# Norms row by row, and a second layer's first operands made on chip, in a hybrid encoder layer

## The chip, the cores and the metric

The kernel runs on one core of a Trainium2 chip. The metric is the device time of one execution in microseconds (us), lower is better. The program is written in a tile framework: Python generators issue instructions, the framework fixes at build the order of each engine's instructions, near to the order in which the generators are stepped, and adds the waits. The engines are TensorE (PE in the profile; PEld its weight loads), the vector engine (DVE), ScalarE (ACT), GpSimd (POOL), and SyncE's queue (SP), which issues nearly all DMAs and, in order, waits for what each transfer needs.

## The reference

One layer over two sequences (512 and 1024 rows of 1024 numbers), with alpha = 2^0.25:

```python
x = layer_norm(ALPHA * x + 0.5 * swiglu(x, ffn1_wg, ffn1_wu, ffn1_wd), ln_g[0], ln_b[0])
x = layer_norm(ALPHA * x + hybrid_mixer(x, w_in, ..., w_out), ln_g[1], ln_b[1])
x = layer_norm(ALPHA * x + 0.5 * swiglu(x, ffn2_wg, ffn2_wu, ffn2_wd), ln_g[2], ln_b[2])

def swiglu(x, wg, wu, wd):            # 1024 -> 2816 -> 1024
    return (silu(x @ wg) * (x @ wu)) @ wd

def hybrid_mixer(h, ...):
    rx, rgate, q, k, v, fx = split(h @ w_in)
    out_a = gelu(rgate) * bidir_rglru(conv(rx))
    out_b = diff_attention(q, k, v)             # four heads, two maps each
    out_c = fourier_mix(fx)                     # Re of a 2-D DFT per channel group
    return concat(out_a, out_b, out_c) @ w_out
```

`layer_norm` subtracts a row's mean, divides by the root of its variance plus 1e-5, multiplies by a gain and adds a bias, all over the 1024 numbers of a row. Everything is fp32.

## The kernel before

The 1536 rows are 12 row tiles of 128 x 1024. The FFNs work in two halves of 6 row tiles; the mixer in three chunks of 4 (chunk 0 is the first sequence). Rows between the parts (`x1` after FFN1, `x2` after the mixer) lie in DRAM.

**Products.** An fp32 product is three matmuls on a high and a low part of each operand (`mm3`, L138). `split` makes the parts: ScalarE casts the high one (L132), the vector engine subtracts it (L133).

**An FFN (`ffn`, L321 on)** makes 11 passes over the 2816 hidden columns, 256 in each, once for each half. A pass has 14 up products: the gate (m = 0) and the up weight (m = 1) in Strassen's scheme of seven products over quarters (`up`). The products' right operands are sums of transposed quarters of the half's rows, 7 operands in three column blocks, made in 21 steps by `seven`: a vector sum, 4 transposes into an accumulator bank (L263), a split. FFN1's first half makes them on chip from its input (`operands`). For each other half they are staged: 21 stores into DRAM (`operands_to`), then loads into the six "xt" slots (`operands_from`). The left operands are sums of weight blocks, made by the vector engine in a first pass of each half (`Weights.made`), three products ahead (`PREP`); from the second pass of the second half on they are loaded, as made in the first half (`kept`, two by two). The down products (`down`, `down_seven`) of a pass stand between the up products of the next.

**The norms.** `layer_norm` (L210 on) takes rows in batches of up to four: means, squares with their sum on ScalarE (L225), one small vector step (L227), a power -0.5 on GpSimd (L228); then for each row (x + mean) * gain on the vector engine (L231); then for odd rows the scale and bias in one vector multiply (L238), and for even rows a scale on ScalarE (L235) and an addition on GpSimd (L236). A first half's norm runs in the second half's first pass, in two batches of three; a second half's runs at the end behind each row's last down product, row by row.

**The mixer (L1209 on).** `project` multiplies by `w_in`; its left columns are transposes of `x1` rows (`columns`; chunk 0's were staged at the end of FFN1, chunks 1 and 2 load their rows from DRAM). Then come the recurrence and, block by block, the attention, beside which `others` is stepped: the rest of `project`, the Fourier parts (`fnet`) of both sequences, the output projections (`out_proj`) of chunks 0 and 1 and the norm of chunk 0. At the end stand, in this order:

```python
norm(1, accs[1])
run(islice(staging, len(SEVEN)))
for _ in self.out_proj(2, chunk(x1, 2), accs[2]):
    next(staging, None)
run(staging)
norm(2, accs[2])
```

where `staging` loads the rows of `x2` that FFN2's first half needs ("p" slots), makes its operands and stores them. An output projection has 16 output tiles, each of 24 matmuls of 256 columns, drained by the vector engine into the residual rows, which are in "x" slots (six in all); the norm of chunk 1 works on four of them.

Of the kernel before, what the change touches and what calls it, by code (L numbers as in the profile page):

```python
# [67 lines left out]
STREAM = 2  # L68
DOWN_AT = (0, 1, 3, 4, 6, 8, 9, 11)
# [33 lines left out]
class Kernel:  # L103
# [137 lines left out]


# [78 lines left out]
    def ffn(self, n, which, src, dst, scr, wscr, first=False, beside=iter(()), staged=iter(()), meanwhile=iter(())):  # L321
# [108 lines left out]

        def out(m, got, i, j, x, result):
# [80 lines left out]
        def norm(half, accs, parts):  # L512
            params = self.ln_params(which, "p")
            for part in parts:
                self.layer_norm(accs, sums[:, half] if half else sums[:, half, :, :1], params, dst[half * HALF:(half + 1) * HALF], part)
                yield
# [15 lines left out]
        def kept(todo):  # L532

            slots, views = [], []

            def ahead(n=STREAM):
                while todo and len(slots) < n:
                    w = self.slot("w", [2, 2, h, P], F32R)
                    nc.sync.dma_start(f32(w), f32(todo.pop(0)))
                    slots.append(w)  # L540
# [10 lines left out]

        def first_pair(raws, rooms):
# [4 lines left out]
        ready = iter(())  # L557
        if first:
            rows = self.load_rows(src[:HALF], "x")
            raws = load(0)  # L560
            _, store, operand = self.operands()
            ready = self.seven(lambda r: rows[r::3], store, [(k, r) for k in SEVEN for r in range(3)], nc.gpsimd)
        else:
            raws = load(0)
# [5 lines left out]
        staging = self.operands_to(self.pairs(src[HALF:]), scr[1], [(k, r) for r in range(3) for k in SEVEN])  # L570
# [7 lines left out]
        with self.phase(f"ffn{n}a", FFN_SLOTS, FFN_BANKS):  # L578
            run(islice(ready, 6))
            for p in range(NP):  # L580
# [5 lines left out]
                else:  # L586
                    products = both(first_pair(raws, [[t[:, 0], t[:, 1]] for t in (self.slot("p", [2, h, P]) for _ in raws)]), got, "h")
# [8 lines left out]
                if p == 0:  # L596
                    accs = self.load_rows(src[:HALF], "x")
# [5 lines left out]
            operand = self.operands_from(scr[1])  # L603
# [3 lines left out]
        norms = norm(0, accs, [range(0, 3), range(3, 6)])  # L607
        get, ahead = kept([wscr[p][:, c:c + 2] for p in range(1, NP) for c in range(0, 2 * len(SEVEN), 2)])

        def between():  # L610
            if p == 0:
                next(norms, None)
            if STAGE <= p:
                next(staging, None)

        with self.phase(f"ffn{n}b", LATE_SLOTS, LATE_BANKS):
            steps = iter(())
            for p in range(NP):
                got = {}
                result = "a" if p == NP - 1 else None  # L620
                if p:
                    fifth = lambda: self.slot("d", [HT])
                    products = chain(*(up(m, get, got, between, result, fifth) for m in range(2)))
                else:
                    products = both(first_pair(raws, [[self.slot(t, [h, P]) for t in "bd"] for _ in raws]), got, result)
# [19 lines left out]
            norms = norm(1, accs, [range(t, t + 1) for t in last])  # L645
            for t in last:
                next(meanwhile, None)
                down(got, ws, t, True)
                next(norms)
            run(meanwhile)  # L650

# [490 lines left out]
    def run(self):  # L1142
        tc, nc, ins = self.tc, self.nc, self.ins
        with ExitStack() as ctx:
# [45 lines left out]
            scr = [[[dram.tile([P, KD // 2, 2, HT], F32R, name=f"ops{n}{i}{k}") for k in SEVEN] for i in range(2)] for n in range(2)]  # L1190
# [107 lines left out]
```

## Time and profile before

| | us |
|---|---|
| three runs, median | 2902.63 (2901.74 to 2905.0) |
| the profiled execution, its own time | 2902.0 |
| its span | 2899.9 |
| TensorE busy | 2762.1 (95%) |
| vector engine busy | 1929.5 (67%) |
| ScalarE busy | 1157.9 (40%) |
| GpSimd busy | 135.1 (5%) |

The mean granted TensorE clock is 0.976 of full speed. The span is what the profiler saw between the first and the last instruction; the execution's own time has 2.1 us more. Busy times are unions over an engine's instructions, and a wait is put down to the semaphore that came last. On the time axis FFN1's first half ends at about 546 us, FFN1 at 1070, the attention's first sequence lies from about 1410 to 1530, the mixer ends at 1859 with FFN2's first pass behind it, and FFN2's second half begins at about 2383.

### The profile page before, as it was taken

How to read it: one execution, taken by the hardware profiler on the slowest of the kernel's cores; microseconds unless marked ns; L12 is line 12 of the kernel's file. 1: busy time of each engine (PE TensorE's matmuls, PEld its weight loads, DVE VectorE, ACT ScalarE, POOL GpSimd, SP SyncE). 2: the span in 40 equal slices, each digit the busy share in tenths (PEclk: the TensorE clock that was granted, in tenths of full speed). 3: DMA queues.
4: the chain of work that ended last, by engine and by line, in shares of the span. 5: the costliest groups of instructions: out<-in, count | busy, mean ns of one | idle time of the engine just before them, and what ended most of it. 6: DMA issues, size and time to landing. Idle time of an engine off the chain costs nothing. (4 is left out here: it accounts for less than half of the span.)

```text
span 2899.9 us, 39216 instructions
## 1 busy us (share of the span) xinstructions
PE 2762.1 (95%) x14940; PEld 2521.3 (87%) x14940; DVE 1929.5 (67%) x3217; ACT 1157.9 (40%) x2093; POOL 135.1 (5%) x106
## 2 busy tenths in 40 slices
PE   8999999899999989999889986899999998999997
PEld 7999999799999978978678976799999998999996
DVE  7677666677676672453477754667766667676776
ACT  5344334333332344662365642344443334323223
POOL 2000000100000020000000011100000001000002
PEclk9999999999999999999899998899999999999999
DMA  7799766878555572244585486988876586555552
GB/s 255 267 317 317 281 239 227 302 282 271 198 183 193 183 241 83 96 159 141 171 235 153 136 277 216 339 291 303 296 280 242 211 310 221 201 187 191 190 186 104
DMA packets 318076, 650.48 MB, mean 224 GB/s; under 512 B 22976, under 2 KB 194624, under 8 KB 297408
## 3 DMA queue, kind: packets, MB, share of 16 engines
q1 hardware_dynamic: 313888, 641.16, 64.0%
q0 software_dynamic: 4000, 6.82, 0.9%
q8 instruction: 117, 1.92, 0.3%
q14 instruction: 71, 0.58, 0.1%
HBM read 403.06 MB, written 244.84 MB: 223 GB/s over the span
## 5 line engine op out<-in xcount | busy, mean ns | idle before, releaser
L138 PE MATMUL up<-xt,a 128*128 128x384 f32 x4032 | 746.8, 340 | 36.9 <-ACT a L132 27.3
L138 PEld LDWEIGHTS up<-xt,a 128*128 128x128 f32 x4032 | 710.8, 190 | 52.5 <-ACT a L132 31.8
L138 PE MATMUL up<-xt,w 128*128 128x384 f32 x3360 | 617.9, 337 | 0.0
L138 PEld LDWEIGHTS up<-xt,w 128*128 128x128 f32 x3360 | 588.6, 188 | 22.3 <-ACT t L422 10.0
L138 PE MATMUL big<-w,h 128*128 128x512 f32 x1584 | 387.1, 393 | 0.5 <-ACT h L132 0.2
L509 DVE SCALAR_TENSOR_TENSOR x<-big,x 128x512 f32<-128x512 f32 x420 | 277.7, 685 | 111.7 <-PE big L138 109.0
L138 PEld LDWEIGHTS big<-w,h 128*128 128x128 f32 x1584 | 295.3, 188 | 58.7 <-ACT h L132 1.6
L138 PE MATMUL big<-a,h 128*128 128x512 f32 x1260 | 317.9, 394 | 0.0
L138 PEld LDWEIGHTS big<-a,h 128*128 128x128 f32 x1260 | 234.0, 188 | 40.7
L138 PE MATMUL big<-xt,w 128*128 128x512 f32 x1008 | 234.3, 392 | 0.0
L456 DVE SCALAR_TENSOR_TENSOR x<-big,x 128x1024 f32<-128x1024 f32 (+1 forms) x156 | 177.2, 1138 | 81.0 <-PE big L138 78.5
L138 PEld LDWEIGHTS big<-xt,w 128*128 128x128 f32 x1008 | 189.7, 189 | 40.2 <-ACT x L961 0.4
L133 DVE TENSOR_TENSOR a<-w,a 128x512 fp32r<-128x512 f32 x244 | 166.2, 698 | 50.2 <-ACT a L132 48.4
L132 ACT CAST a<-w 128x512 fp32r<-128x512 f32 x244 | 147.6, 621 | 22.3 <-DMA w<-in_ffn_wg 14.0
L132 ACT CAST a<-b 128x512 fp32r<-128x512 f32 x168 | 103.8, 620 | 122.0 <-PE up L138 50.5
L133 DVE TENSOR_TENSOR a<-b,a 128x512 fp32r<-128x512 f32 x168 | 114.9, 688 | 42.9 <-ACT a L132 40.5
L132 ACT CAST h<-t 128x384 fp32r<-128x384 f32 x168 | 86.2, 513 | 119.5 <-DVE t L439 72.3
L138 PE MATMUL mm<-w,xt 128*128 128x256 f32 x960 | 122.4, 285 | 1.3 <-DVE x L1136 1.3
L138 PEld LDWEIGHTS mm<-w,xt 128*128 128x128 f32 x960 | 118.2, 193 | 2.0 <-DVE x L1136 1.9
L403 DVE TENSOR_TENSOR t<-t,up 128x384 f32<-128x384 f32 x88 | 48.7, 553 | 91.7 <-ACT t L402 91.3
L422 ACT COPY t<-up 128x384 f32<-128x384 f32 x88 | 42.2, 479 | 166.6 <-PE up L138 166.4
L414 ACT COPY t<-up 128x384 f32<-128x384 f32 x88 | 42.2, 479 | 161.8 <-PE up L138 161.8
(309 smaller groups left out, 3129.8 us busy)
## 6 DMA issues: line engine op xcount, KB each, us to landing
left<-a SPq DMA_DIRECT2D x280, 512.0 KB, 4.2
w<-left SPq DMA_DIRECT2D x140, 1024.0 KB, 4.7
ops<-a SPq DMA_DIRECT2D x63, 512.0 KB, 4.2
x<-x SPq DMA_DIRECT2D x52, 512.0 KB, 4.3
w<-in_ffn_wg SPq DMA_DIRECT2D x24, 1024.0 KB, 5.8
w<-in_ffn_wu SPq DMA_DIRECT2D x24, 1024.0 KB, 7.4
d<-in_ffn_wd SPq DMA_DIRECT2D x88, 256.0 KB, 4.5
w<-in_ffn_wd SPq DMA_DIRECT2D x20, 1024.0 KB, 5.0
```

The costliest lines, as they stand in the source:

```text
L132: self.nc.scalar.copy(hi, src)
L133: self.nc.vector.tensor_sub(lo, src, f32(hi))
L138: self.nc.tensor.matmul(out, lhs(l), rhs(r), start=first and n == 0, stop=last and n == 2, skip_group_check=onto)
L403: nc.vector.tensor_add(s, s, b)
L414: nc.scalar.copy(s, a)
L422: nc.scalar.copy(s2 := quarter(), a)
L456: nc.vector.scalar_tensor_tensor(accs[t][:, at], pd, scale, accs[t][:, at], op0=ALU.mult, op1=ALU.add, **acc)
L509: nc.vector.scalar_tensor_tensor(x, ps, scale, x, op0=ALU.mult, op1=ALU.add)
```

## The change

1. **Norms row by row.** `layer_norm_row` does one row in three steps, all multiplies on the vector engine, and `layer_norm_rows` interleaves neighbours. It is used for both halves of both FFNs and for chunks 1 and 2. Chunk 0's norm stays a batch.
2. **FFN2's first operands on chip.** Rows 0 to 3 of `x2` are loaded into the mixer's "m" slots, rows 4 and 5 are those of chunk 1 in their "x" slots. 18 of the 21 steps of `seven` are stepped with chunk 2's output projection, three in FFN2's first pass. Chunk 1's norm goes row by row beside that projection (rows 2, 3, 0, 1), chunk 2's goes along with FFN2's first pass (`extra`).
3. **The FFNs' end.** The last pass's up products for m = 1 go in the order 1, 2, 3, 4, 5, 0, 6 (`up_late`), the rows' last down products in the order 3, 4, 5, 0, 1, 2, and the first of them comes before the last up products.
4. **FFN1 into the mixer.** FFN1's last six rows stay in their slots (`held`); of chunk 1 only rows 4 and 5 are loaded, into "a" slots.
5. **Fourier.** The first step of each `fnet` (loads and vector folds) is stepped earlier, between the steps of `project`.
6. Rooms for weight sums are in "b" and "d" slots in the first halves too (before: "p"), and the mixer's norm parameters in "p" (before: "x").

```diff
+    def layer_norm_row(self, a, sums, params, dst):
...
+        nc.vector.tensor_scalar(mean, sums, -1.0 / D, None, op0=ALU.mult)
+        nc.scalar.activation(self.slot("a", [D], BF16), a, AF.Square, bias=mean, accum_out=var)
+        yield
+        nc.vector.tensor_scalar(var, var, 1.0 / D, EPS / ALPHA ** 2, op0=ALU.mult, op1=ALU.add)
+        nc.gpsimd.tensor_tensor(rs, var, self.mhalf[:, :1], op=ALU.pow)
+        nc.vector.scalar_tensor_tensor(a, a, mean, params[0], op0=ALU.add, op1=ALU.mult)
+        yield
+        nc.vector.scalar_tensor_tensor(a, a, rs, params[1], op0=ALU.mult, op1=ALU.add)
+        nc.sync.dma_start(dst, a)
+        yield
+    def layer_norm_rows(self, rows, params):
+        late = iter(())
+        for x in rows:
+            row = self.layer_norm_row(*x[:2], params, x[2])
+            next(row)
+            next(late, None)
+            yield
+            next(row)
+            late = row
+            yield
+        next(late, None)
+        yield
@@ ffn @@
+        def ending(got, ws):
+            norms = norm(1, accs, last)
+            for t in last:
+                down(got, ws, t, True)
+                next(norms)
+                next(norms)
+                next(meanwhile, None)
+                yield
+            run(norms)
-        if first:
+        if start is None:
...
-            operand = self.operands_from(scr[0])
+            operand, ready, extra = start
...
-        last = (3, 0, 1, 2, 4, 5)
+        last = (3, 4, 5, 0, 1, 2)
@@ first half, first pass @@
                 for i, _ in enumerate(products):
+                    if not p:
+                        next(extra, None)
                     if not p and i % 2:
                         run(islice(ready, 3))
@@ second half @@
-        norms = norm(0, accs, [range(0, 3), range(3, 6)])
+        norms = norm(0, accs, last)
...
                 for i, _ in enumerate(products):
+                    if p == 0:
+                        next(norms, None)
                     if i in DOWN_AT:
                         next(steps, None)
+                    if p == NP - 1 and i == 12:
+                        run(steps)
+                        rest = ending(got, ws)
+                        next(rest)
@@ run @@
-            xts = [self.columns_from(cols)] + [self.columns(lambda c=c: self.load_rows(chunk(x1, c), "x")) for c in range(1, NCH)]
+            held = []
+            xts = [self.columns_from(cols), self.columns(lambda: self.load_rows(x1[TPC:HALF], "a") + held[:2 * TPC - HALF]),
+                   self.columns(lambda: held[2 * TPC - HALF:])]
@@ mixer @@
-        order = [(k, r) for r in range(3) for k in SEVEN]
-        staging = self.operands_to(self.pairs(x2[:HALF]), scr, order)
-        others = Steps(project, self.fnet(0, SEQS[0]), self.fnet(1, SEQS[1]),
+        fnets = [self.fnet(q, S) for q, S in enumerate(SEQS)]
+        others = Steps(islice(project, 15), begun(fnets[0]), project, islice(fnets[0], 3), begun(fnets[1]), *fnets,
                        self.out_proj(0, chunk(x1, 0), None, beside=x1p), first_norm(),
                        self.out_proj(1, chunk(x1, 1), accs[1]))
         along(self.attention(blocks[0] + blocks[1], dist, others), others, PACE)
-        norm(1, accs[1])
-        run(islice(staging, len(SEVEN)))
-        for _ in self.out_proj(2, chunk(x1, 2), accs[2]):
-            next(staging, None)
-        run(staging)
-        norm(2, accs[2])
+        rows = self.load_rows(x2[:TPC], "m") + accs[1][:HALF - TPC]
+        params = self.ln_params(1, "p")
+        norms = norm(1, accs[1], params, (2, 3, 0, 1))
+        _, store, operand = self.operands()
+        ready = self.seven(lambda r: rows[r::3], store, [(k, r) for k in SEVEN for r in range(3)], nc.vector)
+        for n, _ in enumerate(self.out_proj(2, chunk(x1, 2), accs[2])):
+            next(norms, None)
+            if n >= 8:
+                run(islice(ready, 1 + n % 2))
+        run(norms)
+        return operand, ready, norm(2, accs[2], params)
```

**Where the order moves.** First TensorE, from the end of chunk 2's output projection (`mm<-w,xt`) over the transposes of the operands (`big<-ident`) into FFN2's first pass (`up`) with the first down products behind it (`big<-w,h`). Before:

```order
L263 MATMUL big<-ident,p 128x128 x4
L138 MATMUL mm<-w,xt 128x256 x24
L263 MATMUL big<-ident,p 128x128 x4
L138 MATMUL mm<-w,xt 128x256 x144
L138 MATMUL up<-xt,a 128x384 x168
L138 MATMUL big<-w,h 128x512
L138 MATMUL up<-xt,a 128x384 x2
```
With the change:

```order
L139 MATMUL mm<-w,xt 128x256 x24
L297 MATMUL big<-ident,x 128x128 x8
L139 MATMUL up<-xt,a 128x384 x24
L297 MATMUL big<-ident,m 128x128 x8
L139 MATMUL up<-xt,a 128x384 x12
L297 MATMUL big<-ident,m 128x128 x4
L139 MATMUL up<-xt,a 128x384 x98
L139 MATMUL big<-w,h 128x512
L139 MATMUL up<-xt,a 128x384 x70
L139 MATMUL big<-w,h 128x512 x11
```
The last transposes stood before 144 matmuls of the projection, and the first pass followed without a break; now transposes stand between the projection's last tiles and the first up products, 12 of them within the first pass.

Then the vector engine, in the first pass of FFN1's second half: the norm's multiplies (`x<-x,st,p`: L231, L238; with the change L256, L258), splits of left operands (`a<-b`, `a<-d`), weight sums (`b<-w,d`) and the products' evictions (`t`). Before:

```order
L231 SCALAR_TENSOR_TENSOR x<-x,st,p 128x1024 x2
L227 TENSOR_SCALAR st<-st 128x3
L231 SCALAR_TENSOR_TENSOR x<-x,st,p 128x1024
L238 SCALAR_TENSOR_TENSOR x<-x,st,p 128x1024
L133 TENSOR_TENSOR a<-b,a 128x512
L231 SCALAR_TENSOR_TENSOR x<-x,st,p 128x1024 x2
L227 TENSOR_SCALAR st<-st 128x3
L231 SCALAR_TENSOR_TENSOR x<-x,st,p 128x1024
L238 SCALAR_TENSOR_TENSOR x<-x,st,p 128x1024 x2
L133 TENSOR_TENSOR a<-b,a 128x512
L133 TENSOR_TENSOR a<-d,a 128x512 x2
```
With the change:

```order
L256 SCALAR_TENSOR_TENSOR x<-x,st,p 128x1024
L134 TENSOR_TENSOR a<-b,a 128x512
L134 TENSOR_TENSOR a<-d,a 128x512
L258 SCALAR_TENSOR_TENSOR x<-x,st,p 128x1024
L437 TENSOR_TENSOR t<-t,up 128x384
L410 TENSOR_TENSOR b<-w,d 128x512
L254 TENSOR_SCALAR st<-st 128x1
L256 SCALAR_TENSOR_TENSOR x<-x,st,p 128x1024
L437 TENSOR_TENSOR t<-t,up 128x384
L134 TENSOR_TENSOR a<-d,a 128x512
L507 TENSOR_TENSOR t<-t 128x384
L134 TENSOR_TENSOR a<-b,a 128x512
```
Before, three multiplies of a batch stand together, and the small step that needs all three squares (128x3) stands between them; now each row has its own small step, and other work stands between the multiplies.

Last SP's queue, where FFN1's last rows are stored and the mixer's first columns begin (`x_6_126` and the like are rows of `x1` in DRAM, `rx` a projection's output). Before:

```order
L160 DMA x<-x_4_124 128x1024
L144 DMA a<-in_w_in 128x8x128
L240 DMA x_6_126<-x 128x1024
L160 DMA x<-x_5_125 128x1024
L240 DMA x_7_127<-x 128x1024
L144 DMA r<-in_w_in 128x8x128
L240 DMA x_8_128<-x 128x1024
L160 DMA x<-x_6_126 128x1024
L240 DMA x_10_130<-x 128x1024
L160 DMA x<-x_7_127 128x1024
L679 DMA rx_76<-d 128x512
L240 DMA x_11_131<-x 128x1024
```
With the change:

```order
L259 DMA x_11_131<-x 128x1024
L145 DMA a<-in_w_in 128x8x128
L145 DMA r<-in_w_in 128x8x128
L259 DMA x_6_126<-x 128x1024
L145 DMA r<-in_w_in 128x8x128
L259 DMA x_7_127<-x 128x1024
L772 DMA rx_76<-d 128x512
L161 DMA a<-x_4_124 128x1024
L161 DMA a<-x_5_125 128x1024
L259 DMA x_8_128<-x 128x1024
L772 DMA rx_76<-b 128x512
```
The loads of chunk 1's rows into "x" slots (four, between the stores) are now two, of rows 4 and 5 into "a" slots, and stand behind the store of the first projected columns.

## Rows read from the trace of the kernel before

**Rows 1.** Page, part 1: busy time, share of the span, instructions, whole execution.

```profile
PE 2762.1 (95%) x14940; PEld 2521.3 (87%) x14940; DVE 1929.5 (67%) x3217; ACT 1157.9 (40%) x2093; POOL 135.1 (5%) x106
```

**Rows 2.** Windows: length, busy (x) PE PEld DVE ACT POOL, PEclk, DMA share, GB/s.

```profile
546.50:589.00 42.50, 33.47 (x170) 31.46 (x170) 33.87 (x42) 22.65 (x40) 13.43 (x7) 0.84 0.66 249
1030.00:1076.00 46.00, 37.06 (x175) 31.18 (x174) 40.72 (x70) 21.55 (x29) 18.94 (x10) 0.93 0.58 190
1410.00:1470.00 60.00, 46.06 (x257) 38.49 (x256) 39.49 (x100) 31.39 (x70) 3.27 (x4) 0.83 0.70 189
1470.00:1530.00 60.00, 49.03 (x271) 40.13 (x269) 41.44 (x85) 34.07 (x62) 3.69 (x4) 0.95 0.83 248
1719.40:1898.40 179.00, 140.92 (x1023) 137.30 (x1022) 91.86 (x165) 55.01 (x87) 15.24 (x6) 0.88 0.80 269
2383.00:2425.40 42.40, 33.40 (x170) 31.52 (x169) 34.05 (x43) 23.17 (x41) 12.21 (x5) 0.84 0.66 258
2450.00:2850.00 400.00, 400.00 (x2095) 371.60 (x2094) 277.08 (x476) 119.28 (x233) 0.00 (x0) 1.00 0.53 187
```

**Rows 3.** Timeline of PE, end of the mixer: start, us, instructions, [idle before <-releaser].

```profile
1719.35 31.92 PE L138 MATMUL mm<-w,xt 128*128 128x256 f32 x264
...
1766.55 1.04 PE L263 MATMUL big<-ident,p 128*128 128x128 f32 x8
...
1782.80 3.66 PE L263 MATMUL big<-ident,p 128*128 128x128 f32 x16 [8.87 <-DVE a L133]
...
1803.78 1.94 PE L263 MATMUL big<-ident,p 128*128 128x128 f32 x8 [14.28 <-DMA p<-x]
```

**Rows 4.** Chain that ended last, in order of time, FFN2's second half.

```profile
2465.33 8.51 PE up L138 x48
```

**Rows 5.** Timeline of PE, first pass of FFN2.

```profile
1858.98 1.65 PE L138 MATMUL up<-xt,a 128*128 128x384 f32 x4 [6.17 <-ACT a L132]
1863.65 1.65 PE L138 MATMUL up<-xt,a 128*128 128x384 f32 x4 [3.02 <-ACT a L132]
```

**Rows 6.** Page, part 6: DMA issues; KB each, median us from issue to landing.

```profile
ops<-a SPq DMA_DIRECT2D x63, 512.0 KB, 4.2
x<-x SPq DMA_DIRECT2D x52, 512.0 KB, 4.3
```

**Rows 7.** Groups by line and shape, ACT, 542.5:589 (busy us, mean ns).

```profile
L225 ACT ACTIVATE a<-x,st 128x1024 bf16<-128x1024 f32 x6 | 6.9, 1146 | 0.0
L235 ACT ACTIVATE x<-x,st 128x1024 f32<-128x1024 f32 x3 | 3.3, 1146 | 5.8 <-POOL st L228 5.8
```

**Rows 8.** Timeline of all engines, last rows' norms.

```profile
2889.57 2.80 POOL L228 TENSOR_TENSOR st<-st,mhalf 128x1 f32<-128x1 f32 x2
...
2892.37 2.34 POOL L236 TENSOR_TENSOR x<-x,p 128x1024 f32<-128x1024 f32 x1
2892.40 3.39 DVE L238 SCALAR_TENSOR_TENSOR x<-x,st,p 128x1024 f32<-128x1024 f32 x1 [0.44 <-POOL st L228]
```

**Rows 9.** Timeline of DVE, end of FFN1: a drain and a multiply.

```profile
1039.91 0.69 DVE L456 SCALAR_TENSOR_TENSOR x<-big,x 128x512 f32<-128x512 f32 x1 [0.41 <-PE big L138]
...
1042.77 1.28 DVE L238 SCALAR_TENSOR_TENSOR x<-x,st,p 128x1024 f32<-128x1024 f32 x1
```

**Rows 10.** Groups by line and shape, DVE, 542.5:589 (busy us, mean ns).

```profile
L231 DVE SCALAR_TENSOR_TENSOR x<-x,st,p 128x1024 f32<-128x1024 f32 x6 | 9.9, 1663 | 1.8 <-ACT a L225 1.8
L238 DVE SCALAR_TENSOR_TENSOR x<-x,st,p 128x1024 f32<-128x1024 f32 x3 | 6.0, 2014 | 1.6 <-POOL st L228 1.6
...
L133 DVE TENSOR_TENSOR a<-d,a 128x512 fp32r<-128x512 f32 x5 | 3.3, 685 | 0.7 <-ACT a L132 0.7
```

**Rows 11.** Timeline of PE, attention over the first sequence, Fourier matmuls.

```profile
1420.87 2.41 PE L138 MATMUL big<-p,x 128*128 128x256 f32 x12 [1.55 <-DMA p<-chan]
...
1449.64 0.58 PE L138 MATMUL big<-x,w 128*128 128x256 f32 x1 [4.78 <-ACT w L132]
```

**Rows 12.** Timeline of PE, the mixer's first transposes.

```profile
1070.07 2.18 PE L153 MATMUL big<-ident,x 128*128 128x128 f32 x9 [6.29 <-ACT d L678]
```

More of the change, by code (lines that the diff above doesn't have):

```diff
@@ L240, in layer_norm @@
                     STORE(nc, t).dma_start(dst[t], a)
+    def layer_norm_row(self, a, sums, params, dst):
+        nc = self.nc
+        st = self.tiny("st", [3, TPC])
+        mean, var, rs = (st[:, i, :1] for i in range(3))
+        if sums.shape[1] > 1:
+            nc.vector.tensor_reduce(mean, sums, axis=mybir.AxisListType.X, op=ALU.add)
+            sums = mean
+        nc.vector.tensor_scalar(mean, sums, -1.0 / D, None, op0=ALU.mult)
[20 more added lines that the diff above has]
+        yield
     def seven(self, rows, store, order, add):
@@ L318, in pairs, with ffn @@
         return get
-    def ffn(self, n, which, src, dst, scr, wscr, first=False, beside=iter(()), staged=iter(()), meanwhile=iter(())):
+    def ffn(self, n, which, src, dst, scr, wscr, start=None, beside=iter(()), staged=iter(()), meanwhile=iter(())):
         nc = self.nc
@@ L429, in up, with up_late @@
             yield
+        def up_late(m, w, got, between, result, fifth):
+            a = self.psum("up", [CH])[:, :HT]
+            product(a, w(), 1)
+            s = quarter()
+            nc.scalar.copy(s, a)
+            yield
+            c = self.psum("up", [CH])[:, :HT]
+            product(c, w(), 2)
+            p5 = fifth()
+            nc.scalar.copy(p5, c)
+            yield
+            product(a, w(), 3, True)
+            s1 = quarter()
+            nc.scalar.copy(s1, a)
+            yield
+            product(c, w(), 4, True)
+            nc.vector.tensor_add(s1, s1, c)
+            out(m, got, 0, 1, s1, result)
+            yield
+            product(a, w(), 5, True)
+            nc.scalar.copy(s2 := quarter(), a)
+            nc.vector.tensor_add(s2, s2, p5)
+            out(m, got, 1, 1, s2, result)
+            yield
+            b = self.psum("up", [CH])[:, :HT]
+            product(b, w(), 0)
+            nc.vector.tensor_add(s, s, b)
+            out(m, got, 0, 0, s, result)
+            yield
+            product(a, w(), 6, True)
+            out(m, got, 1, 0, a, result)
+            yield
         def out(m, got, i, j, x, result):
@@ L510, in down_seven, with norm @@
                 yield
[L512 to L516, printed above, removed]
+        def norm(half, accs, rows):
+            return self.layer_norm_rows([(accs[t], sums[:, half, t, :2 if half else 1], dst[half * HALF + t]) for t in rows],
+                                        self.ln_params(which, "p"))
         def prepared(todo, keep):
@@ L550, in kept, with rooms @@
             return get, ahead
+        def rooms():
+            return [[self.slot(t, [h, P]) for t in "bd"] for _ in range(2)]
         def first_pair(raws, rooms):
@@ L644, in ffn @@
             run(beside)
[L645 to L649, printed above, removed]
+            run(rest)
             run(meanwhile)
+        return accs
     def project(self, xts):
@@ L1219, in mixer, with norm, begun @@
         accs = [[] for _ in range(NCH)]
[L1221 to L1223 removed]
+        def norm(c, rows, params, part=range(TPC)):
+            return self.layer_norm_rows([(rows[t], self.sums[:, c, t], chunk(x2, c)[t]) for t in part], params)
         def first_norm():
[L1226 removed]
+            self.layer_norm(self.load_rows(x1p, "x"), self.sums[:, 0], self.ln_params(1, "x"), chunk(x2, 0))
             yield
[L1229 to L1231 removed]
+        def begun(steps):
+            next(steps)
+            yield
+        fnets = [self.fnet(q, S) for q, S in enumerate(SEQS)]
+        others = Steps(islice(project, 15), begun(fnets[0]), project, islice(fnets[0], 3), begun(fnets[1]), *fnets,
                        self.out_proj(0, chunk(x1, 0), None, beside=x1p), first_norm(),
```

52 lines of the change are left out of this document (30 added, 22 removed).

## The prediction

> **What bounds the kernel now.** I read the page's busy times first. TensorE is busy for 2762.1 of 2899.9 us, the vector engine for 1929.5 [rows 1]. So TensorE bounds the kernel, and a change that takes no matmul away can only win back time in which TensorE stands still or runs below its full clock. Next I cut the span into stretches. From 2450 to 2850 us, a steady part of FFN2's second half, TensorE is busy for 400.00 of 400 us at a granted clock of 1.00: nothing is to be had there. The losses stand in five places that the change touches: the first passes of both second halves (granted clock 0.84 each), the way from FFN1 into the mixer (0.93), the attention over the first sequence (0.83 and 0.95), and the end of the mixer with FFN2's first pass (0.88) [rows 2]. A stretch's loss is its length less its matmuls at the duration that they have where nothing holds them.
>
> **The end of the mixer and FFN2's first pass (179.0 us).** The stretch holds 1023 TensorE instructions [rows 2]: the output projections of chunks 1 and 2 with 768 matmuls of 256 columns, 168 first up products, 84 transposes, and 3 others. A projection matmul takes 31.92/264 = 0.121 us, a transpose 1.04/8 = 0.13 at full clock [rows 3], an up product 8.51/48 = 0.177 [rows 4]. The work is 92.9 + 29.7 + 10.9 = 133.5 us, and the loss 45.5. Three parts of it have names. TensorE waits 8.87 us for a vector subtraction of the staging, then 14.28 us for rows that come back from DRAM [rows 3]; after the projection it waits 6.17, 3.02 and more for casts of the first pass [rows 5]; at such places a transpose takes 3.66/16 = 0.229 us where 0.13 is its full-clock duration, which is the lower level of 1.2 GHz [rows 3]. The change takes away the wait for the rows (4 of 6 are back before the last projection, 2 never left the chip), 21 staging stores of 4.2 us on SP's queue [rows 6] and the operand loads. The transposes stay, 84 of them; 18 of 21 steps now stand beside the projection, where TensorE has other work behind each.
>
> What remains there after the change:
> - Chunk 2's residual rows 2 and 3 need x slots that chunk 1's rows 2 and 3 give up after their norm and their store. The norm of a row alone takes some 4.6 us: the squares 1.15 [rows 7], the power 2.80/2 = 1.4 [rows 8], a multiply 1.28 [rows 9], small steps 0.8. A store and a load of 4.2 and 4.3 [rows 6] and a drain of 0.69 [rows 9] follow, so the third tile's accumulator is free after 13.8. TensorE needs it after four tiles of 24 matmuls, 4 x 24 x 0.121 = 11.6. That is a wait of 2 to 3 us; I take 2.8. The Trainium skill's page "DMA: Bandwidth & Descriptors", section "Anatomy of one DMA — SWDGE (gpsimd) path", has a fixed 2.0 us plus the bytes over 436e3, an estimate of 3.2 us for 512 KB, by which this wait would be gone and the time 2 us lower; it speaks of GpSimd's path, and the SP rows here show 4.2 and 4.3.
> - Two to three us of transposes that wait for one of the three accumulator banks.
> - FFN2's first pass is paced by the vector engine: between the last drain and the last split it has 8 multiplies (10.2 us by 1.28 [rows 9]) and some 25 splits, sums and products of at most 0.69 [rows 10], together at most 27.5, with 2 to 4 of waits for ScalarE, against 29.7 of matmuls, of which the first can't begin at once: a loss of 2 to 4.
> - About 2 us of work at the lower clock, and the splits of operand 5, whose memory the projection's last matmuls still read, so that they start only behind it; its transposes are among the last, and this I put into the 2 to 4.
>
> That is a rest of 10 to 13 us, so a gain of **33**. The worst end keeps the later waits as they are (6.17 + 3.02 and a like one) beside the rest: 45.5 - 21.5 = 24. The best end keeps 7.5: 38.
>
> **The first passes of the two second halves (42.5 and 42.4 us).** In each, 168 up products by 0.177 are 29.7 us, so 12.8 are lost [rows 2, 4]. The vector engine there does 6 + 3 multiplies of the norms in 9.9 + 6.0 us, 1.66 and 2.01 us each [rows 10], where one alone takes 1.28 [rows 9]: GpSimd's adds run beside the slow ones. It also waits 1.8 and 1.6 us for the batch's squares and power [rows 10]. Row by row all 12 multiplies are on the vector engine, 12 x 1.28 = 15.4 against 15.9: no more than before. The batch's two waits, 3.4 us, have other rows in front of them, and 3 of the 12 multiplies (3.8 us) now stand behind the last split of a left operand, where TensorE has its products. 3.4 + 3.8 + 0.5 = 7.7; the norms' backlog that this pushes into the second pass, ahead of its first down product, takes a little back. I take **7 each**; bounds 4 (the slow multiplies alone, 15.9 - 9 x 1.28) and 11 (a loss of 2 is left). ScalarE loses three scales of 1.15 [rows 7], and GpSimd its adds; nothing waits for these. Here too FFN1's first half takes other rooms for weight sums; 36 up products of the next pass cover the loads of down weights that this delays (0, +-1).
>
> **The Fourier folds begun sooner.** In the attention over the first sequence TensorE waits 1.55 us for a table and 4.78 for a split [rows 11]; the folds' vector work and the table's load move ahead of both. That is 6.3, and 0.7 for clock: **7**. Below it 0, if the operand tiles, held longer, make other loads wait; above 12, if the stretch's matmuls (46.06 us at 0.83, some 39 at full clock [rows 2]) also get half of the clock back. The total of steps beside attention is the same, so the later places in it don't move.
>
> **The way from FFN1 into the mixer.** Rows 6 to 11 stay on chip, and chunk 1's rows 4 and 5 are loaded. Their loads stand on SP's queue behind a store that waits for a ScalarE copy; the transposes begin now at 1070.07, after a 6.29 us wait for that kind of copy [rows 12]. With three scales of 1.15 fewer in front of it [rows 7] the copy comes some 2 us sooner, the load lands 4.3 [rows 6] behind it: 2.3 later than now. I take **-2**, from -6 (a row of stores more) to +2 (the rows come first). The loads that go, and the new order of FFN1's last products, lie beside matmuls.
>
> **The end.** The last multiply takes 3.39 us beside a GpSimd add of 2.34 [rows 8]; alone 1.28, so 2.1 come back. Three more multiplies, 3.8 us, come onto the same engine in the last rows: **-2**; from -4 to 0.
>
> **The sum** is 33 + 7 + 7 + 7 - 2 - 2 = 50. The profiled execution took 2902.0 us, its span 2899.9; the median shown is 2902.63, 0.6 above. 2902.0 - 50 = **2852.0**. The bounds together: 24 + 4 + 4 + 0 - 6 - 4 = 22 gives 2880, and 38 + 11 + 11 + 12 + 2 + 0 = 74 gives 2828.
>
> **The rivals.** *The vector engine takes the waits over.* It is busy for 33.87 of 42.5 us in a first pass [rows 2], and with every norm on it each gap that closes on one side opens on the other. Then the first passes gain nothing, at the end of the mixer only the two staging waits go, less the new 2.8 (8.87 + 14.28 - 2.8 = 20.3), and the Fourier part brings 5: 20.3 + 5 - 4 = 21, so 2881. For it speaks that this engine's backlog has to be worked off somewhere; against it, that its work does not grow.
>
> *All gaps close.* 40 + 12.8 + 12.8 + 12 - 4 = 73.6: 2828. Against it: three engines hand every operand on.
>
> *The change doesn't do what it says.* If the shared memory holds the operands back until the projection ends, the splits queue on the vector engine behind the one that waits, and the end of the mixer gains 5 and the first passes 2 each: 9 - 4 = 5, so 2897, no change.
>
> *Slower: the clock falls to 1.2 GHz in the three first passes.* Row by row there are more and shorter waits instead of few long ones. At the lower level a pass takes twice its 29.7, 89 us for three: 2852 + 89 = 2941. It decides from (2908 - 2852)/89 = 63% of the three passes at the lower level. For it speaks that the first passes have 0.84 now; against it, that waits of a few us in the second half of the first sequence's attention leave 0.95 [rows 2]. The Trainium skill's page "TensorE: Matmul & The Clock Gate", section "A second HAM failure mode: psum-queue depth-cycling", says that short idles between groups of matmuls can make the clock swing between its two levels; by that rule this rival would be the likely one, and the 0.95 speaks against it.
>
> **How the numbers follow.** The forecast gets 0.53, the vector engine as the bound 0.25, all gaps closed 0.12, no effect 0.05, the clock 0.05. The range goes from 2828 (the sum's better bound and the second rival) to 2882 (the worse bound, and the first rival with it). A measurement of this kernel can tell a difference from no change above some 0.2%, 5.8 us. The first three cases are faster: 0.90; same 0.05; slower 0.05.
>
> **What would show it.** Right: no row of TensorE that waits for rows from DRAM between the projections and FFN2; the first passes of the second halves near 30 to 36 us with a clock near 0.95 and multiplies of 1.28; no GpSimd adds in the second halves; a wait at the mixer's entry for the load of row 4; the wait of 4.78 gone. Wrong: a long vector backlog after a first pass with TensorE waiting for casts there, a new wait on a residual row over 5 us in the last projection, or a lower clock in those passes than 0.84.

## The result, and the profile after

The changed kernel takes 2836.24 us (median of 4 runs, 2833.67 to 2837.2), the kernel before 2902.18 us (4 runs) beside it. The ratio is 0.9769, 95% interval 0.9753 to 0.9786: faster by 66 us, where 50 were forecast. The range held it; two terms of the sum did not stay within their own bounds (the end of the mixer and FFN2's second half, both better).

Page, part 1, of the changed kernel:

```profile
PE 2747.3 (97%) x14940; PEld 2512.1 (89%) x14940; DVE 1926.3 (68%) x3279; ACT 1141.4 (40%) x2089; POOL 116.7 (4%) x104
```

Against [rows 1] TensorE has the same 14940 matmuls in 14.8 us less of busy time, so that part of the gain is clock; the other 51.5 of the 66.3 us of span (2899.9 to 2833.6) are standing time.

Windows of the changed kernel: FFN1's second half, its first pass and the start of its second; the attention over the first sequence; the end of the mixer with FFN2's first pass; and the first pass of FFN2's second half (columns as in [rows 2]).

```profile
547.30:576.60 29.30, 29.30 (x170) 29.27 (x169) 26.05 (x43) 18.04 (x35) 12.01 (x7) 1.00 0.85 313
576.60:596.90 20.30, 16.56 (x80) 14.76 (x78) 17.33 (x28) 7.50 (x16) 2.49 (x3) 0.92 0.96 356
1400.00:1460.00 60.00, 49.91 (x284) 42.49 (x284) 40.20 (x101) 31.97 (x73) 3.29 (x4) 0.91 0.74 206
1460.00:1520.00 60.00, 49.38 (x263) 40.20 (x262) 41.22 (x85) 33.77 (x59) 3.67 (x4) 0.91 0.79 231
1708.90:1847.00 138.10, 134.63 (x1040) 133.35 (x1039) 93.03 (x205) 53.87 (x99) 11.25 (x8) 1.00 0.60 206
2329.30:2358.70 29.40, 29.40 (x170) 29.06 (x169) 25.84 (x42) 17.95 (x34) 10.63 (x5) 1.00 0.80 284
```

Both first passes have closed: 29.30 and 29.40 us, all busy at 1.00, for 42.5 and 42.4 at 0.84 [rows 2]. But behind the first of them 20.30 us hold only 16.56 of work. The end of the mixer is 138.10 us with 1040 instructions, 134.63 busy at 1.00.

To see where time came from I cut each profile at the same instructions of TensorE: the first up product of a second half, the first `w_in` product in the mixer, the second pair of the attention's score products (behind the recurrence), the last small matmul ahead of chunk 1's output projection, the last matmul. The lengths (us; differences of start times in the timeline, good to 0.2; "tail" is from the last matmul's end to the span's end):

| kernel | FFN1 first half | FFN1 second half | into the mixer, recurrence | attention | end of mixer, FFN2 first half | FFN2 second half | tail |
|---|---|---|---|---|---|---|---|
| before | 546.9 | 504.9 | 246.4 | 420.9 | 663.9 | 500.6 | 16.2 |
| changed | 547.5 | 496.1 | 247.8 | 417.3 | 620.7 | 488.1 | 16.1 |
| changed, again | 548.9 | 496.1 | 248.5 | 414.0 | 619.2 | 488.3 | 16.1 |
| n1 batch, GpSimd | 548.7 | 500.8 | 248.9 | 413.0 | 621.5 | 498.1 | 16.1 |
| n2 rows, GpSimd | 552.7 | 503.1 | 249.2 | 412.9 | 620.7 | 494.0 | 16.0 |
| n11 batch, no GpSimd | 548.0 | 499.8 | 248.3 | 413.4 | 621.3 | 497.8 | 16.1 |
| n3 over DRAM | 550.5 | 494.7 | 248.5 | 416.6 | 638.2 | 487.8 | 16.1 |
| n4 norm ahead | 547.5 | 494.8 | 248.4 | 416.0 | 621.6 | 488.1 | 16.1 |
| n12 steps sooner | 549.3 | 496.4 | 247.5 | 414.1 | 625.1 | 488.0 | 16.1 |
| n5 Fourier late | 547.5 | 496.3 | 249.0 | 423.1 | 622.2 | 488.0 | 16.1 |
| n6 tables later | 552.5 | 491.2 | 248.6 | 415.9 | 623.4 | 487.9 | 16.1 |
| n7 rows 4, 5 sooner | 548.9 | 496.0 | 247.6 | 414.2 | 621.4 | 488.1 | 16.1 |
| n9 old end | 550.9 | 497.2 | 247.9 | 411.2 | 620.6 | 487.9 | 16.1 |
| n10 two more edits | 547.6 | 491.2 | 244.3 | 414.0 | 620.2 | 488.0 | 16.1 |

Of the 66.3 us the end of the mixer and FFN2's first half give 43.2, the second halves 8.8 and 12.5, the attention 3.6 and the tail 0.1; 0.6 are lost in FFN1's first half and 1.4 on the way into the mixer. Stages that a kernel leaves alone spread by 1 to 6 us, so a stage is judged against all the profiles that share its code.

### The profile page after: what moved, and what is told of

Its sections match the earlier page's. It is cut to its first block, busy times and chain, and to the rows that moved or that the text cites. A ratio compares the mean times of both kernels' runs of the same rounds, so it can differ in the third digit from the quotient of the medians.

```text
span 2833.6 us, 39167 instructions
## 1 busy us (share of the span) xinstructions
PE 2747.3 (97%) x14940; PEld 2512.1 (89%) x14940; DVE 1926.3 (68%) x3279; ACT 1141.4 (40%) x2089; POOL 116.7 (4%) x104
## 5 line engine op out<-in xcount | busy, mean ns | idle before, releaser
L139 PE MATMUL up<-xt,a 128*128 128x384 f32 x4032 | 735.2, 338 | 8.1 <-DVE a L134 3.1
L139 PEld LDWEIGHTS up<-xt,a 128*128 128x128 f32 x4032 | 703.2, 188 | 19.6 <-DVE a L134 4.2
L134 DVE TENSOR_TENSOR a<-b,a 128x512 fp32r<-128x512 f32 x176 | 122.1, 697 | 41.1 <-ACT a L133 38.3
L255 POOL TENSOR_TENSOR st<-st,mhalf 128x1 f32<-128x1 f32 x32 | 55.0, 1721 | 1547.6 <-DVE st L254 1547.6
L456 ACT COPY t<-up 128x384 f32<-128x384 f32 x86 | 41.2, 479 | 155.9 <-PE up L139 155.9
```

The lines of the kernel that those rows point to most:

```text
L134: self.nc.vector.tensor_sub(lo, src, f32(hi))
L139: self.nc.tensor.matmul(out, lhs(l), rhs(r), start=first and n == 0, stop=last and n == 2, skip_group_check=onto)
L255: nc.gpsimd.tensor_tensor(rs, var, self.mhalf[:, :1], op=ALU.pow)
L456: nc.scalar.copy(s2 := quarter(), a)
```

## The experiments

Each is the changed kernel with an edit; the diffs are cut to their main lines (`...`). Totals are medians of 4 or 5 runs beside the kernel before on the same chip.

**Norms in batches again, in the two first passes (n1).**

```diff
-        norms = norm(0, accs, last)
...
+            for part in (range(3, 6), range(3)):
+                self.layer_norm(accs, sums[:, 0, :, :1], params, dst[:HALF], part)
...
```

> The changed kernel with one part undone: in the first passes of both second halves the first half's norm runs again in two batches of three rows, even rows finished by a ScalarE scale and a GpSimd addition. Theory (the norms row by row are what opened these two passes; 7.4 us came there in FFN1 and 12.5 in FFN2): the time goes from 2836 up by about 20 us to 2856 (2848 to 2862), a first pass takes 40 us or more at a granted clock near 0.84, and the vector multiplies there have means of 1.6 to 2.0 us again. Rival (the gain there comes from the other parts, such as the order of the last down products and the rooms): 2832 to 2841.

2847.92 us, ratio 0.9805 (0.9789 to 0.9822). FFN2's second half is 10.0 us longer, FFN1's 4.7: less than the 20 expected, but the greater part of FFN2's 12.5. The pass of 40 us at a clock near 0.84 came (below); the slow multiplies did not. In that pass they take 1.28 us:

```profile
L232 DVE SCALAR_TENSOR_TENSOR x<-x,st,p 128x1024 f32<-128x1024 f32 x6 | 7.6, 1278 | 0.0
L239 DVE SCALAR_TENSOR_TENSOR x<-x,st,p 128x1024 f32<-128x1024 f32 x3 | 3.8, 1279 | 0.8 <-POOL st L229 0.8
```

The batches come in another order here than before (rows 3 to 5 first), and GpSimd's additions fall beside splits, of which one takes 2.84 us instead of 0.69:

```profile
2349.03 3.45 POOL L237 TENSOR_TENSOR x<-x,p 128x1024 f32<-128x1024 f32 x1 [1.27 <-ACT x L236]
2350.19 2.84 DVE L134 TENSOR_TENSOR a<-b,a 128x512 fp32r<-128x512 f32 x1
```

**Row by row, but GpSimd for even rows (n2), and batches without GpSimd (n11).** The diff is n2's; n11 is n1 with the second multiply of every row on the vector engine.

```diff
...
+        if pooled:
+            nc.scalar.activation(a, a, AF.Identity, scale=rs)
+            nc.gpsimd.tensor_add(a, a, params[1])
...
```

> The changed kernel with norms row by row, but in the first passes of the two second halves the even rows are finished by a ScalarE scale and a GpSimd addition, as before. Theory A (what cost was the GpSimd addition beside the vector engine, which lengthens its multiplies): 2844 to 2852, the multiplies' means 1.5 to 2.0 us there. Theory B (what cost was the batch, whose rows all wait for the last row's squares and for the power, with the multiplies in one block ahead of the splits): 2834 to 2841, with first passes still near 30 us though single multiplies are longer.

> As n1_batch (batches of three in the first passes of both second halves), but all rows are finished on the vector engine, with no ScalarE scale and no GpSimd addition. It parts what n1_batch and n2_pool left together. If GpSimd's addition is the larger cost (FFN2's second half was 5.9 us longer with it row by row, 10.0 us with batches too), FFN2's second half is 2 to 5 us longer than in the changed kernel, 490 to 493 us, and the total 2839 to 2843. If the batch is the larger cost, 495 to 498 and 2845 to 2848.

n2: 2847.36 us (0.9804, 0.9789 to 0.9819). n11: 2846.48 us (0.98, 0.9787 to 0.9813). Windows of the first pass of FFN2's second half in n1, n2 and n11:

```profile
2332.70:2372.70 40.00, 34.85 (x169) 33.49 (x168) 34.23 (x43) 22.84 (x41) 13.59 (x5) 0.83 0.66 253
```

```profile
2338.50:2370.00 31.50, 29.45 (x170) 29.10 (x169) 28.22 (x42) 20.53 (x37) 16.98 (x8) 1.00 0.64 227
```

```profile
2330.70:2370.30 39.60, 34.40 (x170) 33.43 (x169) 34.24 (x48) 20.06 (x38) 3.51 (x2) 0.87 0.80 307
```

The vector engine's multiplies in that pass by line and shape, in n2 and then n11:

```profile
L256 DVE SCALAR_TENSOR_TENSOR x<-x,st,p 128x1024 f32<-128x1024 f32 x6 | 10.5, 1743 | 0.0
L262 DVE SCALAR_TENSOR_TENSOR x<-x,st,p 128x1024 f32<-128x1024 f32 x3 | 3.8, 1275 | 0.0
```

```profile
L232 DVE SCALAR_TENSOR_TENSOR x<-x,st,p 128x1024 f32<-128x1024 f32 x6 | 7.5, 1281 | 0.0
L239 DVE SCALAR_TENSOR_TENSOR x<-x,st,p 128x1024 f32<-128x1024 f32 x6 | 7.3, 1280 | 0.7 <-POOL st L229 0.7
```

n2 has the slow multiplies (1743 ns) and yet a pass of 31.50 us at full clock; n11 has none (1281 ns) and takes 39.60. So what lengthens this pass is the batch: its block of multiplies stands ahead of the left operands' splits. The vector engine's and TensorE's timelines in n11 show it (the wait of 3.58 us is for the split at 2357.20), and the clock falls to 0.87 with it:

```profile
2350.03 3.67 DVE L232 SCALAR_TENSOR_TENSOR x<-x,st,p 128x1024 f32<-128x1024 f32 x3
2353.61 3.67 DVE L239 SCALAR_TENSOR_TENSOR x<-x,st,p 128x1024 f32<-128x1024 f32 x3
2357.20 0.69 DVE L134 TENSOR_TENSOR a<-b,a 128x512 fp32r<-128x512 f32 x1
```

```profile
2357.94 12.47 PE L139 MATMUL up<-xt,a 128*128 128x384 f32 x54 [3.58 <-DVE a L134]
```

GpSimd's addition has a price of its own, but mostly behind the pass: n2's whole half is 5.9 us longer, 2.1 of it in the pass, and then TensorE waits for a split of `h` and for the drain of a residual row:

```profile
2376.64 1.90 PE L139 MATMUL big<-a,h 128*128 128x512 f32 x7 [1.31 <-DVE h L134]
...
2386.04 0.96 PE L139 MATMUL big<-a,h 128*128 128x512 f32 x3 [1.92 <-DVE x L581]
```

With batches, n1 against n11, it changes next to nothing (498.1 and 497.8): the additions lengthen three splits by 4.8 us in all, but three multiplies (3.8 us) are off the vector engine. No run here has batches with slow multiplies, as before. For FFN2's half n11's second case, that the batch is the larger cost, came with both of its numbers; n2's total lies in the range of its theory A, its pass as theory B had it.

In FFN1's half the order is the other way round: n2 is 7.0 us longer, n11 3.7. There Fourier tables pass through slots that the second pass needs (n6, below). In n2 their store is late, and TensorE waits for it; in n11 and n1 the tables' waits are gone behind the longer pass:

```profile
599.82 0.56 DVE L543 TENSOR_TENSOR b<-t 128x384 f32<-128x384 f32 x1 [6.94 <-DMA dft<-b]
600.98 1.65 PE L139 MATMUL big<-a,h 128*128 128x512 f32 x3 [6.48 <-ACT h L133]
```

Against n6, which has no such wait, n11 is 8.6 us longer in this half and n1 9.6, close to FFN2's 9.7 and 10.0. In the total n2 and n11 cost the same.

**FFN2's operands over DRAM (n3), norm 1 ahead (n4), steps from the start (n12).**

```diff
-        ready = self.seven(..., store, ..., nc.vector)
+        ready = self.operands_to(lambda r: rows[r::3], scr, ...)      # n3
+        run(norms)                                                    # n4, ahead of out_proj(2)
-            if n >= 8:
-                run(islice(ready, 1 + n % 2))
+            next(ready, None)                                         # n12
```

> The changed kernel with FFN2's first operands made at the same places from the same rows on chip, but stored to DRAM and loaded again into the operand slots, as before. Theory (the way over DRAM is a good part of the 43 us won at the end of the mixer: the last stores of 4.2 us, then loads that start only when the slots are free, then products): 15 to 25 us slower than the changed kernel, 2851 to 2861, with a wait of TensorE for operand loads ahead of FFN2's first pass. Rival (all of it comes from the norm beside the projection and from rows that need not be loaded): 2834 to 2842.

> The changed kernel with chunk 1's norm issued whole ahead of chunk 2's output projection, still row by row; the operands stay on chip. Theory (the norm beside the projection matters, because the projection's weight splits stand behind the norm's multiplies on the vector engine): 6 to 12 us slower, 2842 to 2848, with TensorE waiting for weight splits between the two projections. Rival (only the round trip over DRAM mattered; the weights are split in time anyway): 2834 to 2840.

> The changed kernel, but the steps that make FFN2's first operands are stepped one by one from the beginning of chunk 2's output projection, and not from its second quarter on. Theory (the two waits of 8.87 and 14.28 us before came from the place of the transposes on TensorE's queue, ahead of projection tiles that were ready, while their rows were not): TensorE waits for rows again, 6 to 15 us in the projection, 2842 to 2851. Rival (the rows are there early enough now, since two never leave the chip and four come without a norm in between): 2834 to 2839.

n3: 2854.35 us (0.9829, 0.9814 to 0.9844), the stage 17.5 us longer. All 21 steps stand ahead of FFN2 here. TensorE's timeline, and the vector engine's ahead of the first of these waits, where a load of FFN2's weights is late:

```profile
1816.27 1.97 PE L297 MATMUL big<-ident,m 128*128 128x128 f32 x8 [4.30 <-DVE a L134]
1821.11 7.49 PE L139 MATMUL up<-xt,a 128*128 128x384 f32 x30 [2.87 <-ACT a L133]
1831.69 1.52 PE L139 MATMUL up<-xt,a 128*128 128x384 f32 x5 [3.10 <-DMA xt<-opsf]
```

```profile
1813.45 0.69 DVE L404 TENSOR_TENSOR b<-w 128x512 f32<-128x512 f32 x1 [4.32 <-DMA w<-in_ffn_wu]
```

n4: 2837.21 us (0.9768, 0.9752 to 0.9785), the stage 0.9 longer, which is within its spread: the time is the rival's. But the edit did not bring the norm ahead of the projection. In the trace its multiplies still stand between the drains of chunk 2's first tiles, and the last begins 3.7 us sooner than in the changed kernel (1767.80); so what a norm ahead of the projection would cost stays open:

```profile
1757.11 0.42 DVE L1229 SCALAR_TENSOR_TENSOR x<-mm,x 128x256 f32<-128x256 f32 x1
1757.51 1.27 DVE L256 SCALAR_TENSOR_TENSOR x<-x,st,p 128x1024 f32<-128x1024 f32 x1
...
1764.13 1.28 DVE L258 SCALAR_TENSOR_TENSOR x<-x,st,p 128x1024 f32<-128x1024 f32 x1
```

n12: 2839.89 us (0.9777, 0.9762 to 0.9792), between theory and rival; its interval overlaps the changed kernel's. The stage is 4.4 longer, 1.7 above the longest of the other profiles that share it (623.4, n6), with waits of 1.80 and 1.73 us in the projection: the place of the transposes seems to count, but for less than expected. So of the 43.2 us the way over DRAM, with what it does to the queue, has 17.5. That the rows need no load behind a store was not undone alone, and no run puts the other 26 us down to a part.

**Fourier parts at their old place (n5).**

```diff
-        others = Steps(islice(project, 15), begun(fnets[0]), project, islice(fnets[0], 3), begun(fnets[1]), *fnets,
+        others = Steps(project, *fnets,
```

> The changed kernel without the earlier begin of the Fourier parts (their first steps stand where they stood before). Theory (the earlier folds gave the 3 to 4 us by which the attention over the first sequence became shorter, and the waits of 1.55 and 4.78 us return): 2838 to 2842. Rival (that gain is the noise of other waits, or the slots held longer cost as much as they gave): 2833 to 2837.

2844.01 us (0.9792, 0.9779 to 0.9806), more than the 3 to 4 us that were expected. The attention takes 423.1 us. In the 12 other profiles with the folds begun sooner it takes 411.2 to 417.3, median 414.05; the changed kernel's first profile is the highest of them. So this part is worth some 7 (420.9 - 414.05) to 9 us (423.1 - 414.05; one profile each of the longer length), and the wait, which is gone in both profiles of the changed kernel, is back:

```profile
1445.70 1.68 PE L139 MATMUL big<-x,w 128*128 128x256 f32 x4 [4.78 <-ACT w L133]
```

**Tables a pass later (n6).** FFN1's second half gave less than FFN2's. In the changed kernel TensorE waits here at the start of its second pass, and the vector engine ahead of it for a store:

```profile
586.70 2.33 PE L139 MATMUL big<-a,h 128*128 128x512 f32 x9 [1.74 <-ACT h L133]
591.03 3.92 PE L139 MATMUL big<-a,h 128*128 128x512 f32 x9 [2.00 <-ACT h L133]
```

```profile
585.54 0.56 DVE L539 TENSOR_TENSOR b<-t 128x384 f32<-128x384 f32 x1 [0.81 <-DMA dft<-b]
```

Fourier tables pass through the two "b" slots there, which the sums of `down_seven` need next.

```diff
+                if p:
-                next(beside, None)
+                    next(beside, None)
```

> The changed kernel, but the step that copies two Fourier tables through the two b slots is left out after the first pass of FFN1's second half and comes a pass later. Theory (FFN1's first pass gave 7.4 us where FFN2's gave 12.5, because there the second pass's sums wait for the b slots until the tables are stored): 4 to 5 us faster, 2831 to 2833, and no wait of TensorE for the first splits of h in the second pass (1.74 and 2.00 us in the changed kernel). Rival (the difference is the vector engine's backlog of norms): within 1 us of the changed kernel, 2835 to 2838.

The half takes 491.2 us, 4.9 less (and again in n10), and the waits are gone but for 0.24. The total does not show it clear of noise (2833.86 us, 0.976, 0.9741 to 0.9779; runs from 2829.26 to 2840.73): in the profile FFN1's first half, which the edit leaves alone, took 5.0 longer.

**Rows 4 and 5 sooner (n7), and both edits with "m" slots (n10).** The mixer's first transposes in the changed kernel, and SP's queue ahead of them:

```profile
1063.08 3.67 PE L154 MATMUL big<-ident,a 128*128 128x128 f32 x16 [8.47 <-DMA a<-x]
```

```profile
1056.31 0.34 SPq L259 DMA_DIRECT2D x<-x  x1
1056.94 0.34 SPq L772 DMA_DIRECT2D rx<-d  x1
1057.32 1.85 SPq L161 DMA_DIRECT2D a<-x  x2
```

```diff
             with self.phase("mixer", MIXER_SLOTS, MIXER_BANKS):
+                held += self.load_rows(x1[TPC:HALF], "a")      # n7; "m" in n10
```

> The changed kernel, but the loads of chunk 1's rows 4 and 5 are issued at the beginning of the mixer, ahead of the recurrence's constants, and not behind the store of the first projected columns. Theory (the wait of 8.47 us ahead of the mixer's first transposes is that of the queue): 4 to 7 us faster, 2829 to 2833; what is late next is the copy of a projected block on ScalarE, behind the squares of the last rows. Rival (the two slots held longer delay the projection's weights by as much): 2834 to 2840.

> The changed kernel with two things more: the two Fourier tables after the first pass of FFN1's second half are copied a pass later (as in n6_tables), and chunk 1's rows 4 and 5 are loaded into two m slots at the beginning of the mixer, far ahead on the queue. Theory: FFN1's second half is 4.9 us shorter than in the changed kernel, as n6_tables showed; the wait of 8.47 us ahead of the mixer's first transposes goes, and there the next to be late is the ScalarE copy of a projected block, so 3 to 6 us more: 2826 to 2830. Rival (the two m slots held longer delay the weights' splits or the distances): the way into the mixer is as long as now, 2831 to 2833.

n7: 2834.56 us (0.9758, 0.9744 to 0.9772); the way into the mixer is 247.6 us, no shorter than the changed kernel's 247.8 and 248.5, so the rival's time came. Here are n7's queue and transposes:

```profile
1057.87 0.34 SPq L259 DMA_DIRECT2D x<-x  x1
1058.26 1.44 SPq L161 DMA_DIRECT2D a<-x  x2
```

```profile
1064.14 2.18 PE L154 MATMUL big<-ident,a 128*128 128x128 f32 x9 [8.16 <-DMA a<-x]
```

The loads passed the `rx` store, but still stand behind the store of a norm's row, probably because the framework gave them a place by their "a" slots. With "m" slots (n10) they go out at 1023.13, ahead of the row stores (the next at 1030.14), and the next to be late are the two copies:

```profile
1051.66 1.09 PE L154 MATMUL big<-ident,m 128*128 128x128 f32 x8 [0.88 <-ACT d L772]
...
1057.48 1.75 PE L154 MATMUL big<-ident,x 128*128 128x128 f32 x7 [4.73 <-ACT b L772]
```

n10 takes 2826.06 us (2823.57 to 2832.89), ratio 0.9737 (0.9724 to 0.9751), as expected: FFN1's second half 4.9 us shorter, the way in 3.5. It has the lowest median here; its gain over the changed kernel, 7 to 10 us by the medians, agrees with these 8.4.

**The old end of the halves (n9), and the changed kernel again.**

```diff
-                    forms = (up, up) if p < NP - 1 else (up, up_late)
+                    forms = (up, up)
```

with all last down products behind the up products.

> The changed kernel with the old end of the FFNs' second halves: the last pass's products in their old order, all down products of the last rows behind them; norms row by row in the order 3, 4, 5, 0, 1, 2 as in the change. Theory (the new end gave 1.3 us at FFN1 and hides the vector engine's three more multiplies at the end of FFN2): 2 to 5 us slower, 2838 to 2842. Rival (it lies beside matmuls, as the prediction had it): 2834 to 2838.

> The changed kernel once more, for the spread of its stages from one profile to the next. In the runs so far FFN1's first half took 547 to 553 us and the attention 411 to 417 in kernels that leave both as they are in the changed kernel. If that is chance of a run, this one gives other lengths than 547.5 and 417.3 us; if it belongs to a kernel's layout, it gives these again within 1 us. The total: 2834 to 2838.

n9: 2835.91 us (0.9765, 0.9752 to 0.9778); FFN1's half 1.1 us longer, FFN2's no different: the rival held, the new end lies beside matmuls. Again (n13): 2833.12 us (0.9758, 0.9745 to 0.9772), just under the 2834 to 2838 expected, with other lengths in the spreading stages (548.9 and 414.0): so these do not belong to the kernel's layout, but to the run, or to the chip that it ran on.

## Why the prediction was right, and where it was not

The waits that were to go went, and the vector engine did not take them over; what was wrong is sizes. Against the forecast the end of the mixer gave 10.2 us more, FFN2's second half 5.5, FFN1's 1.8, the tail 2.1 and the mixer's entry 0.6, and in the first profile the Fourier part 3.4 and FFN1's first half 0.6 less: 16 in all.

**The end of the mixer: the mechanism right, the rest too large.** 33 were forecast, at best 38; the stage gave 43.2. Of the 10 to 13 us that I left as loss, 2.3 are there by the stage's length, and the window above stands still for 3.5 (138.10 - 134.63), which are the three waits below.
- The wait for the residual rows was taken as 2.8 (its own sum, 13.8 - 11.6, gives 2.2), for the third tile. That tile's accumulator was free in time; TensorE waits 0.45 us for the next one's. Here are TensorE, then row 2's store and load, then the third tile's drain, and the fourth's, for which it waits:

```profile
1770.61 0.62 PE L139 MATMUL mm<-w,xt 128*128 128x256 f32 x3 [0.45 <-DVE x L1229]
```

```profile
1757.60 0.34 SPq L259 DMA_DIRECT2D x<-x  x1
...
1761.05 0.34 SPq L161 DMA_DIRECT2D x<-x  x1
```

```profile
1765.06 0.43 DVE L1229 SCALAR_TENSOR_TENSOR x<-mm,x 128x256 f32<-128x256 f32 x1 [0.36 <-DMA x<-x]
...
1770.13 0.42 DVE L1229 SCALAR_TENSOR_TENSOR x<-mm,x 128x256 f32<-128x256 f32 x1
```

  I let row 2's norm begin with the projection's end, but its sums are complete a tile (2.9 us) before it. The load follows the store's issue by 3.45 us, and the drain that waits for it begins 4.0 after that: 7.5 for both. By the fit in the Trainium skill's "DMA: Bandwidth & Descriptors", section "Anatomy of one DMA — SWDGE (gpsimd) path", which is for GpSimd's path, both would take 6.4, an estimate; these rows on SP's queue are longer.
- The 2 to 3 us of transposes that wait for an accumulator bank had no row behind them, and no such wait is there.
- The first pass loses 0.96 and 2.05 us, in my 2 to 4, and the 2 us at the lower clock did not come: 1.00 throughout.

```profile
1810.73 1.49 PE L139 MATMUL up<-xt,a 128*128 128x384 f32 x7 [0.96 <-DVE xt L134]
```

```profile
1844.36 1.85 PE L139 MATMUL up<-xt,a 128*128 128x384 f32 x9 [2.05 <-DVE a L134]
```

**The second halves' first passes: two errors, of opposite sign in one of them.** 7 each were forecast, 11 at best; FFN2's half gave 12.5. I counted the batch's two waits (3.4), multiplies that move behind the last split (3.8), and nothing for the clock. But of the 12.8 lost [rows 2], 33.47 - 29.7 = 3.8 us were work at the lower level, and they came back with the waits. And the cost of the batch was not its two waits (3.4): n11 puts it at 9.7, clock included and GpSimd out of it. The other 2.8 of FFN2's 12.5 are not put down to a part. FFN1's half gave 8.8, because the tables' slots took back 4.9 (n6); the kernel before has no wait there, and I had put the loss down to a backlog of norms.

**Fourier: 7, and 7 to 9 by all the profiles;** the first profile of the changed kernel alone shows 3.6. The bound of 12 does not follow from its own numbers, which give 6.3 + 7/2, some 10.

**The mixer's entry: -2, measured -1.4,** with the wait that was named, for the load of chunk 1's row: 8.47 us where 6.29 stood. But what held the load was not mainly the `rx` store, which goes out at 1056.94, 0.63 behind the store of a norm's row; n7, with the load ahead of it, waits 8.16. And the load takes longer than the 4.3 that I gave it: the transposes begin 5.8 us behind its issue (1057.32 to 1063.08), 5.9 in n7.

**The tail: -2 forecast, 0.1 gained.** The three more multiplies cost nothing: without GpSimd beside them each takes its 1.28 us, the last one too, and it ends 3.8 us before the span does:

```profile
2828.52 1.28 DVE L258 SCALAR_TENSOR_TENSOR x<-x,st,p 128x1024 f32<-128x1024 f32 x1 [0.44 <-POOL st L255]
```

**The rivals.** The vector engine did not take the waits over: 26.05 of 29.30 us in a first pass. "All gaps close" (2828), which got 0.12, came nearest: the time lies 8 us above it and 16 below the forecast, and n10 reaches it. The clock did the opposite of the slower rival: it was granted in full in the two passes that have no waits left, and in FFN2's first pass beside waits of 0.96 and 2.05 us. So the rule of the Trainium skill's "TensorE: Matmul & The Clock Gate", section "A second HAM failure mode: psum-queue depth-cycling", by which short idles would make the clock swing, has no case in the first two, and the third, at 1.00, does not show it.

## What to carry to other kernels

When a wait on the engine that bounds the kernel goes, count the work behind it that ran at the lower clock as well: here 3.8 us beside 9.0 of standing. Work that one engine does for several rows should be interleaved with what the next engine waits for: here the same twelve multiplies in blocks cost 9.7 us in FFN2's half (n11), multiplies lengthened by GpSimd 2.1 in the pass and 3.8 behind it (n2). Where a wait behind the stage hides a cost, as the tables do in FFN1's half, compare with a run that has no such wait. Look in the trace whether an edit moved what it was meant to move: n4's and n7's did so only in part. A stage's length in one profile spreads by a few us where nothing was changed, so a small part is judged by the stage, over all profiles that share its code.

## What was not expected of the hardware

GpSimd's additions lengthened the vector engine's multiplies beside them, from 1275 to 1743 ns on the mean (n2), and still cost TensorE only 2.1 us in that pass (31.50 against 29.40). And the same program's attention took 417.3 us in one profile and 414.0 in another; FFN1's first half, the same in 13 profiles, took from 547.5 to 552.7. Where the chance lies was not settled.
